# Prefetching the residual's base, finishing the last columns in PSUM, and keeping eight weight units instead of six

## The chip, the cores and the metric

One core of a Trainium2 chip runs the whole kernel. The metric is device time in microseconds; the number of a version is the median of its runs. TensorE (PE) does the matmuls into PSUM; VectorE (DVE), ScalarE (ACT) and GpSimd (POOL) do the elementwise work; SP, ACT and POOL issue DMA transfers. Each engine executes its own instructions in order.

## The reference

One layer: a token mixer, a residual with layer norm, a SwiGLU block, and a second residual with layer norm. The change lies in the last two lines of this cut:

```python
x = layer_norm(ALPHA * x + (1.0 + gt_m) * y, ln1_g[l], ln1_b[l])
h = x * (1.0 + sc_f) + sh_f
y = swiglu(h, w_gate[l], w_up[l], w_down[l])        # (silu(h @ w_gate) * (h @ w_up)) @ w_down
x = layer_norm(ALPHA * x + (1.0 + gt_f) * y, ln2_g[l], ln2_b[l])
```

There are 512 tokens of 2048 columns, and the SwiGLU block has 5632 hidden columns. All is float32.

## The kernel before

Each float32 product is done as three matmuls of split operands: a high part, made by ACT as a rounded copy, and a low part, made by VectorE as the difference (`split`, L276 and L277; `mm3`, L241 to L243). The gate and up products and the down product use seven block products instead of eight (`SEVEN`, `DOWN_SEVEN`), so each of the block products `p1 q7 r6 q5 p3 p2 q4` of the down projection has 22 units: 11 row groups `n` by 2 column halves `cc`. A unit is one weight of 128x1024. For each of two token tiles `t` it does 6 matmuls of 512 columns (`dn_mm`), so a unit is a step of 12 matmuls.

The loop over `steps` (at the end of `layer_kernel`) sets the order. At step s it splits the weight of step s + 3 (`prepare`), issues loads some steps ahead (`fetch_behind`, into five buffers `raw`), and does the matmuls of step s (`dn_product`). After each half of a step, six matmuls, it takes one turn of each side generator: every `yield` in `base_side` and `end_side` is one such turn. The split weights have four buffers, so ACT's `whi` for step s + 3 waits until TensorE has finished step s - 1.

`base_side` makes the second residual's left term from `d_z`, the first sublayer's sum that was stored in DRAM: for each of 4 column blocks c it loads two rows `ln` of 512 columns to all partitions and multiplies them by ALPHA (POOL), and for each of 4 token tiles t it loads a tile `z` (`base`), subtracts the mean and multiplies by the scale (VectorE, L1527), and multiplies and adds the rows (POOL, L1530 and L1531). All transfers of it stand in POOL's queue, in the order of the code. `gtf`, the row of gates, is loaded ahead of them (1 MB to all partitions). The 16 base tiles stay until they are joined.

`end_side` first waits until 16 base tiles are there, then loads the eight rows of the final norm and joins and norms columns as the products deliver them: `join` multiplies a column block by the gate, adds the base and takes the statistics; `norm` does two `scalar_tensor_tensor`s and stores.

The last `KEEP` = 6 units (product `q4`, its last 3 row groups, both halves) have buffers of their own. Their matmuls are left out of the loop and done at the end, token tile by token tile and half by half: for t = 0 first half 0 (3 units, 18 matmuls), then half 1, then t = 1. After each the column is joined on VectorE from PSUM into SBUF (L1650 to L1652). After both halves of a t the statistics are combined (`ln_scale`), and the four column blocks are normed: block 0 on ACT and POOL (L1550 to L1552), blocks 1, 2 and 3 on VectorE (L1554 and L1556).

Of the kernel before, what the change touches and what calls it, by code (L numbers as in the profile page):

```python
# [140 lines left out]
def layer_kernel(ctx, tc, ws, wa, wada, xt, x, cin, bada, lbl, ghg, gcq, gckv, ln1c, lnrow, ident, lvm, dist, out):  # L141
# [11 lines left out]
    def heap(name, dt=FT, w=T):  # L153
        return hp.tile([P, w], dt, name=name, tag="h")
# [4 lines left out]
    def big(name, dt=FR):  # L159
        return bp.tile([P, 4, T], dt, name=name, tag="big")  # L160
# [114 lines left out]
    def split(src, hi, lo, engine=nc.vector):  # L275
        nc.scalar.activation(hi, src, AF.Copy)  # L276
        engine.tensor_sub(lo, src, hi.bitcast(FT))  # L277
# [789 lines left out]
    def gate_row(n, name):  # L1067
        r = cp.tile([P, D], FT, name=name, tag="row")
        nc.gpsimd.dma_start(r, d_row[n].rearrange("k p -> (k p)").rearrange("(o d) -> o d", o=1).to_broadcast([P, D]))
        return r  # L1070
# [152 lines left out]
    def piece(w, n):  # L1223

        if isinstance(w, list):
            return w[n]
        return w[0][:, n * T:n * T + T], w[1][:, n * T:n * T + T]
# [67 lines left out]
    def prepare(step):  # L1295

        if step >= len(steps):
            return
        u = steps[step]
        g = u.group  # L1300
        r = raws.pop((g, u.i), None)
        if r is None:
            r = raws[g, OF[u.i]]
            if u.i == "r6":
                raws[g, "kept"] = r
            if u.i not in ("p1", "p2"):
                del raws[g, OF[u.i]]
        u.pair = u.place() if hasattr(u, "place") else W.pair()
        split(r, *u.pair)


    for c in range(4):
# [148 lines left out]

    def dn_mm(u, t):
        (_, n, cc), i = u.group, u.i
        whi, wlo = u.pair
        hi, lo = facts[i, n]
        at = CHAIN[i], cc, t
        fresh = n == 0 and i in FRESH + ("q4",)
        if fresh:
            acc[at] = bank(f"dn{CHAIN[i]}")
        for k in range(2):  # L1470
            s = slice(k * H + t * P, k * H + t * P + P)
            w = slice(k * T, k * T + T)
            mm3(acc[at], hi[:, s], lo[:, s], whi[:, w], wlo[:, w], fresh and k == 0,
                n == NP2 // 2 - 1 and k == 1, f=mmul, skip_group_check=True)

    def dn_product(u):
# [29 lines left out]
                del acc[CHAIN[i], cc, t]  # L1506
            del ps

    ends = []
    done = {}  # L1510
    base = {}

    def base_side():

        for c in range(4):
            rows = [heap(f"ln{n}") for n in range(2)]
            for n in range(2):
                nc.gpsimd.dma_start(rows[n], lnrow[n][:, c * T:c * T + T].to_broadcast([P, T]))
                nc.gpsimd.tensor_scalar_mul(rows[n], rows[n], ALPHA)
            yield  # L1520
            for t in range(NT):
                z = small("base")
                nc.gpsimd.dma_start(z, d_z[t, c])
                for _ in range(6):
                    yield
                base[t, c] = z
                nc.vector.tensor_scalar(z, z, mv1[t][:, 0:1], mv1[t][:, 3:4], op0=OP.subtract, op1=OP.mult)  # L1527
                for _ in range(2):
                    yield
                nc.gpsimd.tensor_mul(z, z, rows[0])  # L1530
                nc.gpsimd.tensor_add(z, z, rows[1])  # L1531
                yield

    st2 = [cp.tile([P, 24], FT, name=f"sf{t}", tag=f"st{t}") for t in range(NT)]
# [1 line left out]

    def join(t, c, y):

        nc.vector.tensor_mul(y, y, gtf[:, c * T:c * T + T])
        yield  # L1540
        nc.vector.tensor_add(y, y, base.pop((t, c)))
        yield
        nc.vector.bn_stats(st2[t][:, c * 6:c * 6 + 6], y)
        done[t, c] = y

    def norm(t, c, mv, on_pool=False, q=None):

        z, g, b = done.pop((t, c)), rows2[0][c], rows2[1][c]
        if on_pool:
            nc.scalar.activation(z, z, AF.Identity, scale=mv[:, 3:4], bias=mv[:, 4:5])  # L1550
            nc.gpsimd.tensor_mul(z, z, g)
            nc.gpsimd.tensor_add(z, z, b)  # L1552
        else:
            nc.vector.scalar_tensor_tensor(z, z, mv[:, 0:1], g, op0=OP.subtract, op1=OP.mult)  # L1554
            yield
            nc.vector.scalar_tensor_tensor(z, z, mv[:, 3:4], b, op0=OP.mult, op1=OP.add)  # L1556
        (q or nc.sync).dma_start(out[t * P:t * P + P, c * T:c * T + T], z)

    def end_side():

        while len(base) < 16:
            yield
        for n in range(2):
            rows2.append([heap(f"l2_{n}_{c}") for c in range(4)])
            for c in range(4):
                nc.gpsimd.dma_start(rows2[n][c], lnrow[2 + n][:, c * T:c * T + T].to_broadcast([P, T]))
        for n in range(8):
            while not ends:
                yield
            for _ in join(*ends.pop(0)):  # L1570
                yield
            yield

        for t in range(2):
            for cc in range(2):
                v = part["V"][:, 2 * cc + t]
                nc.vector.tensor_mul(v, v, gtf[:, (cc + 2) * T:(cc + 3) * T])
                yield
                nc.vector.tensor_add(v, v, base.pop((t, cc + 2)))
                yield  # L1580
        for t in (2, 3):
            mv = ln_scale(st2[t], "mv2")
            for c in range(4):
                for _ in norm(t, c, mv):
                    yield
                yield
        del part["Y"], part["R"]
        for n in range(4):
            while not ends:
                yield  # L1590
            for _ in join(*ends.pop(0)):
                yield
            yield


    KEEP = 6
    for u in steps[len(steps) - KEEP:]:
        u.place = lambda: (lambda w: (w[:, :2].rearrange("p a b -> p (a b)"), w[:, 2:].rearrange("p a b -> p (a b)")))(big("wkeep"))

    gtf = None  # L1600
    for step in range(len(steps)):
        u = steps[step]
        if step + 3 < len(steps):
            prepare(step + 3)
        fetch_behind(step)
        for ahead, do in ((4, factor_tiles), (8, factor_load)):
            if step + ahead < len(steps):
                v = steps[step + ahead]
                if v.group[0] == "dn" and v.group[2] == 0:
                    do(v.i, v.group[1])  # L1610
        last = step >= len(steps) - KEEP
        if u.group[0] == "gu":
            gu_product(u)
            gu_use(u)
        elif not last:
            dn_product(u)
            dn_use(u)
        add_behind(step)
        if not last:
            u.pair = None  # L1620
        if step == 3 * NPRE + 2:
            for t in range(NT):
                side.drain(t)
            assert not hraw
        if u.group[0] == "gu" and u.group[1] >= NPRE and u.i in ("q7", "q5"):

            nc.gpsimd.tensor_copy(pace, acc_copy[0])
            more(1)
        if step == nsteps - 1:
            del m_hi, m_lo  # L1630
            mh = None
            sums.clear()
            xp.release()
            yp = ctx.enter_context(tc.tile_pool(name="tail", bufs=24, side="right", reuse_waits="tile"))
            small = lambda name, dt=FT: yp.tile([P, T], dt, name=name, tag="y")
            for i in "EYVR":
                part[i] = big(i, FT)
            gtf = gate_row(1, "gtf")
            side.add(0, base_side())
            side.add(1, end_side())  # L1640
    side.drain(0)
# [2 lines left out]
    for t in range(2):  # L1644
        for cc in range(2):
            for u in steps[len(steps) - KEEP:]:
                if u.group[2] == cc:
                    dn_mm(u, t)
            ps, y, v = acc.pop(("Y", cc, t)), heap("y"), part["V"][:, 2 * cc + t]
            nc.vector.tensor_mul(y, ps, gtf[:, (cc + 2) * T:(cc + 3) * T])  # L1650
            nc.vector.tensor_add(y, y, v)
            nc.vector.bn_stats(st2[t][:, (cc + 2) * 6:(cc + 3) * 6], y)  # L1652
            done[t, cc + 2] = y
        mv = ln_scale(st2[t], "mv2")
        for c in (0, 1, 2, 3):
            for _ in norm(t, c, mv, c == 0, nc.scalar if c == 0 else nc.sync):
                pass


# [101 lines left out]
```

## Time and profile before

| | |
|---|---|
| median of 3 runs | 2802.89 us (2801.14 to 2803.51) |
| profiled execution | 2800.09 us, span 2798.0 us |
| busy in it | PE 98%, VectorE 73%, ACT 41%, POOL 24% |
| mean granted clock of TensorE | 0.995 |

The span is the time from the first to the last instruction of the profiled execution; all times below count from its start. A busy share is a mean over the whole span. In a timeline, the brackets behind a row give the idle time of the engine before that instruction and what ended it.

### The profile page before, as it was taken

The page shows a single profiled execution, that of the slowest core. Times are in us where ns is not written, and L with a number is a line of the kernel's source. Part 1 is how long each engine was busy: PE and PEld are TensorE (multiplying, and loading weights), DVE is VectorE, ACT ScalarE, POOL GpSimd, SP SyncE. Part 2 cuts the span into 40 slices and gives each one's busy share as a digit, 9 for nine tenths or more (in the row PEclk, how much of TensorE's full clock was granted, in tenths as well). Part 3 has the DMA queues.
Part 4 walks back from the last instruction along what each step waited for, and adds up shares of the span by engine and source line. Part 5 has one row for each costly group of instructions (what it writes and reads, how often), then busy time and mean ns, then how long its engine had stood idle before and what let it go on. Part 6 is the DMA issues. An engine that isn't in the chain of part 4 may idle for free.

```text
span 2798.0 us, 41846 instructions
## 1 busy us (share of the span) xinstructions
PE 2750.3 (98%) x16090; PEld 2421.6 (87%) x16090; DVE 2040.0 (73%) x2892; ACT 1158.3 (41%) x1724; POOL 675.6 (24%) x911
## 2 busy tenths in 40 slices
PE   8999999999999999999999999999999998999997
PEld 6878888888888888788889999999999998887886
DVE  7877687778862678545767777777777776776697
ACT  4334434242322556222236444444444444554453
POOL 0011132433010575421210212221222213443000
PEclk9999999999999999999999999999999999999999
DMA  9866545555984896996945556665556677888774
GB/s 381 310 212 207 167 159 176 173 178 187 320 287 144 231 283 209 271 282 188 282 156 174 182 188 178 190 183 179 197 177 194 174 189 229 274 277 276 242 257 157
DMA packets 179273, 609.85 MB, mean 218 GB/s; under 512 B 23201, under 2 KB 23505, under 8 KB 176001
## 3 DMA queue, kind: packets, MB, share of 16 engines
q1 hardware_dynamic: 126866, 430.18, 44.8%
q0 software_dynamic: 51776, 176.44, 23.5%
q8 instruction: 126, 2.06, 0.3%
q14 instruction: 73, 0.60, 0.1%
q10 hardware_dynamic: 432, 0.57, 0.1%
HBM read 564.09 MB, written 149.70 MB: 255 GB/s over the span
## 4 chain that ended last, share of the span: by engine, by line
PE 90%; DVE 4%; DMA 3%; issue 2%; ACT 1%; POOL 1%; SPq 0%; DVEq 0%; POOLq 0%; ACTq 0%
PE gb L233 6%; PE y L233 6%; PE ga L233 6%; PE V L243 6%; PE V L241 6%; PE V L242 6%; PE qb L233 3%; PE pb L233 3%; PE g L233 3%; PE v L233 3%; PE Y L241 3%; PE Y L243 3%; PE Y L242 3%; PE pa L233 3%; PE early L233 2%; PE dnV L242 2%
## 5 line engine op out<-in xcount | busy, mean ns | idle before, releaser
L277 DVE TENSOR_TENSOR wlo<-raw,whi 128x1024 fp32r<-128x1024 f32 x376 | 468.4, 1253 | 235.4 <-ACT whi L276 235.3
L276 ACT ACTIVATE whi<-raw 128x1024 fp32r<-128x1024 f32 x376 | 397.5, 1058 | 345.2 <-PE dnV L243 132.8
L363 DVE TENSOR_TENSOR wlo<-raw,whi 128x1024 fp32r<-128x1024 f32 (+1 forms) x228 | 284.3, 1250 | 112.3 <-ACT whi L351 111.9
L351 ACT ACTIVATE whi<-raw 128x1024 fp32r<-128x1024 f32 (+1 forms) x228 | 233.7, 1038 | 194.8 <-DVE raw L1086 72.3
L243 PE MATMUL V<-mhi,wlo 128*128 128x256 f32 x1056 | 298.7, 283 | 0.0
L241 PE MATMUL V<-mhi,whi 128*128 128x256 f32 x1056 | 298.6, 283 | 0.0
L242 PE MATMUL V<-mlo,whi 128*128 128x256 f32 x1056 | 298.4, 283 | 0.0
L242 PEld LDWEIGHTS V<-mlo,whi 128*128 128x128 f32 x1056 | 202.2, 191 | 0.0
L241 PEld LDWEIGHTS V<-mhi,whi 128*128 128x128 f32 x1056 | 202.2, 191 | 0.0
L243 PEld LDWEIGHTS V<-mhi,wlo 128*128 128x128 f32 x1056 | 202.2, 191 | 0.0
L241 PE MATMUL Y<-R,whi 128*128 128x256 f32 x704 | 196.1, 279 | 2.2 <-ACT whi L276 2.2
L243 PE MATMUL Y<-R,wlo 128*128 128x256 f32 x704 | 195.6, 278 | 1.8 <-DVE wlo L277 1.8
L242 PE MATMUL Y<-R,whi 128*128 128x256 f32 x704 | 195.7, 278 | 0.0
L242 PE MATMUL dnV<-wlo,fhi 128*128 128x512 f32 x352 | 139.1, 395 | 10.4 <-DVE wlo L277 10.4
L243 PE MATMUL dnV<-whi,flo 128*128 128x512 f32 x352 | 138.7, 394 | 0.0
L241 PE MATMUL dnV<-whi,fhi 128*128 128x512 f32 x352 | 137.9, 392 | 0.2 <-DVE V L1495 0.2
L241 PEld LDWEIGHTS Y<-R,whi 128*128 128x128 f32 x704 | 133.3, 189 | 2.4 <-ACT whi L276 2.4
L243 PEld LDWEIGHTS Y<-R,wlo 128*128 128x128 f32 x704 | 133.0, 189 | 2.2 <-DVE wlo L277 2.2
L242 PEld LDWEIGHTS Y<-R,whi 128*128 128x128 f32 x704 | 133.2, 189 | 0.0
L276 ACT ACTIVATE whi<-wrow 128x1024 fp32r<-128x1024 f32 x80 | 84.4, 1055 | 84.7 <-DVE wrow L1284 84.7
L997 POOL DMA_DIRECT2D sum_dn<-in_ws x132 | 97.1, 816 | 57.9 <-DMA sum_dn<-in_ws 49.6
L233 PE MATMUL ga<-hThi,whi 128*128 128x512 f32 x256 | 102.0, 398 | 0.0
(453 smaller groups left out, 7740.0 us busy)
## 6 DMA issues: line engine op xcount, KB each, us to landing
raw<-in_ws SPq DMA_DIRECT2D x414, 512.0 KB, 5.0
sum_dn<-in_ws POOLq DMA_DIRECT2D x132, 512.0 KB, 8.6
raw<-in_wada SPq DMA_DIRECT2D x128, 512.0 KB, 5.2
raw<-sum_dn SPq DMA_DIRECT2D x88, 512.0 KB, 4.8
rawb<-in_wada SPq DMA_DIRECT2D x22, 1024.0 KB, 12.0
sum_dn<-sum_dn POOLq DMA_DIRECT2D x44, 512.0 KB, 4.9
wrow<-in_ws SPq DMA_DIRECT2D x40, 512.0 KB, 6.6
sum_gu<-in_ws POOLq DMA_DIRECT2D x24, 512.0 KB, 9.4
```

What stands on the lines that cost most here:

```text
L233: mmul(*a, **k)
L241: f(ps, ahi, bhi, start=first, stop=False, **k)
L242: f(ps, ahi, blo, start=False, stop=False, **k)
L243: f(ps, alo, bhi, start=False, stop=last, **k)
L276: nc.scalar.activation(hi, src, AF.Copy)
L277: engine.tensor_sub(lo, src, hi.bitcast(FT))
L351: nc.scalar.activation(hi, src, AF.Copy)
L363: nc.vector.tensor_sub(lo, src, hi.bitcast(FT))
L997: nc.gpsimd.dma_start(d_sum[g, dst], block(g, src), **({"accum_op": OP.add} if add else {}))
```

## The change

There are three parts. The base's loads are issued a column block ahead: those of block 0 at the start of `base_side`, before 16 turns without work, and those of block c + 1 before the arithmetic of block c; `gtf` is loaded behind those of block 1, and each tile takes 5 turns instead of 9. The last products' columns stay in PSUM: the join writes back to the bank that it reads, and the norm's first instruction writes to PSUM too (for block 1 to a fresh bank `n1`), the second to SBUF. And eight units are kept instead of six; the first two have eight tiles of 512 columns from the pool of the base tiles.

```diff
@@ def prepare(step):
-        split(r, *u.pair)
+        if isinstance(u.pair, list):
+            for k, (hi, lo) in enumerate(u.pair):
+                split(r[:, k * T:k * T + T], hi, lo)
+        else:
+            split(r, *u.pair)
@@ def dn_mm(u, t):
-            mm3(acc[at], hi[:, s], lo[:, s], whi[:, w], wlo[:, w], fresh and k == 0,
+            mm3(acc[at], hi[:, s], lo[:, s], *piece(u.pair, k), fresh and k == 0,
@@
+    def base_load(c):
+        rows = [heap(f"ln{n}") for n in range(2)]
+        zs = [small("base") for t in range(NT)]
+        for n in range(2):
+            nc.gpsimd.dma_start(rows[n], lnrow[n][:, c * T:c * T + T].to_broadcast([P, T]))
+        for t in range(NT):
+            nc.gpsimd.dma_start(zs[t], d_z[t, c])
+        return rows, zs
+
     def base_side():
+        rows, zs = base_load(0)
+        for _ in range(16):
+            yield
         for c in range(4):
-            rows = [heap(f"ln{n}") for n in range(2)]
             for n in range(2):
-                nc.gpsimd.dma_start(rows[n], lnrow[n][:, c * T:c * T + T].to_broadcast([P, T]))
                 nc.gpsimd.tensor_scalar_mul(rows[n], rows[n], ALPHA)
-            yield
+            now, nowz = rows, zs
+            if c < 3:
+                rows, zs = base_load(c + 1)
+            if c == 0:
+                gtf.append(gate_row(1, "gtf"))
             for t in range(NT):
-                z = small("base")
-                nc.gpsimd.dma_start(z, d_z[t, c])
-                for _ in range(6):
-                    yield
+                z = nowz[t]
                 nc.vector.tensor_scalar(z, z, mv1[t][:, 0:1], mv1[t][:, 3:4], op0=OP.subtract, op1=OP.mult)
-                for _ in range(2):
-                    yield
-                nc.gpsimd.tensor_mul(z, z, rows[0])
-                nc.gpsimd.tensor_add(z, z, rows[1])
+                yield
+                yield
+                nc.gpsimd.tensor_mul(z, z, now[0])
+                nc.gpsimd.tensor_add(z, z, now[1])
+                base[t, c] = z
+                yield
+                yield
                 yield
@@
-    KEEP = 6
-    for u in steps[len(steps) - KEEP:]:
-        u.place = ...
+    KEEP = 8
+    def keep_big():
+        w = big("wkeep")
+        return [(w[:, k], w[:, 2 + k]) for k in range(2)]
+    def keep_small():
+        return [(small("wkhi", FR), small("wklo", FR)) for k in range(2)]
+    for n, u in enumerate(steps[len(steps) - KEEP:]):
+        u.place = keep_small if n < 2 else keep_big
@@ at the end, for each t and cc
-            ps, y, v = acc.pop(("Y", cc, t)), heap("y"), part["V"][:, 2 * cc + t]
-            nc.vector.tensor_mul(y, ps, gtf[:, (cc + 2) * T:(cc + 3) * T])
+            y, v = acc.pop(("Y", cc, t)), part["V"][:, 2 * cc + t]
+            nc.vector.tensor_mul(y, y, gtf[0][:, (cc + 2) * T:(cc + 3) * T])
             nc.vector.tensor_add(y, y, v)
@@ at the end, for each t
-        for c in (0, 1, 2, 3):
-            for _ in norm(t, c, mv, c == 0, nc.scalar if c == 0 else nc.sync):
-                pass
+        ys = {c: done.pop((t, c)) for c in range(4)}
+        g, b = rows2
+        z = ys[0]
+        nc.scalar.activation(z, z, AF.Identity, scale=mv[:, 3:4], bias=mv[:, 4:5])
+        for c in (1, 2, 3):
+            y = bank("n1") if c == 1 else ys[c]
+            nc.vector.scalar_tensor_tensor(y, ys[c], mv[:, 0:1], g[c], op0=OP.subtract, op1=OP.mult)
+            if c == 1:
+                nc.gpsimd.tensor_mul(z, z, g[0])
+                nc.gpsimd.tensor_add(z, z, b[0])
+                nc.scalar.dma_start(out[t * P:t * P + P, :T], z)
+                o = ys[1]
+            else:
+                o = heap("y")
+            nc.vector.scalar_tensor_tensor(o, y, mv[:, 3:4], b[c], op0=OP.mult, op1=OP.add)
+            nc.sync.dma_start(out[t * P:t * P + P, c * T:c * T + T], o)
```

POOL's queue at the start of the down products, behind the last store of the hidden activations. Before:

```order
L1069 DMA gtf<-d_row 128x2048
L1518 DMA ln_22587<-in_lnrow 128x512
L1519 TENSOR_SCALAR ln_22587<-ln_22587 128x512
L1518 DMA ln_22588<-in_lnrow 128x512
L1519 TENSOR_SCALAR ln_22588<-ln_22588 128x512
L1523 DMA base<-d_z 128x512
L1530 TENSOR_TENSOR base<-base,ln_22587 128x512
L1531 TENSOR_TENSOR base<-base,ln_22588 128x512
```

And with the change:

```order
L1520 DMA ln_22585<-in_lnrow 128x512
L1520 DMA ln_22586<-in_lnrow 128x512
L1522 DMA base<-d_z 128x512 x4
L1532 TENSOR_SCALAR ln_22585<-ln_22585 128x512
L1532 TENSOR_SCALAR ln_22586<-ln_22586 128x512
L1520 DMA ln_22770<-in_lnrow 128x512
L1520 DMA ln_22771<-in_lnrow 128x512
L1522 DMA base<-d_z 128x512 x4
L1069 DMA gtf<-d_row 128x2048
L1543 TENSOR_TENSOR base<-base,ln_22585 128x512
```

Six loads now stand ahead of the first multiply, where a load, a multiply, a load and a multiply stood ahead of the first `z`; `gtf` went from first place to behind twelve loads.

VectorE at the same place, from its last instruction of the gate and up products (the first row) to its first on `base`. Before:

```order
L1441 TENSOR_TENSOR r<-act,r 128x256
L277 TENSOR_TENSOR wlo<-raw,whi 128x1024
L277 TENSOR_TENSOR flo<-raws,fhi 128x512
L277 TENSOR_TENSOR wlo<-raw,whi 128x1024 x2
L277 TENSOR_TENSOR flo<-raws,fhi 128x512
L277 TENSOR_TENSOR wlo<-raw,whi 128x1024
L1527 TENSOR_SCALAR base<-base,mv_11710 128x512
```

And with the change:

```order
L1445 TENSOR_TENSOR r<-act,r 128x256
L277 TENSOR_TENSOR wlo<-raw,whi 128x1024
L277 TENSOR_TENSOR flo<-raws,fhi 128x512
L277 TENSOR_TENSOR wlo<-raw,whi 128x1024 x2
L277 TENSOR_TENSOR flo<-raws,fhi 128x512
L277 TENSOR_TENSOR wlo<-raw,whi 128x1024 x2
L277 TENSOR_TENSOR flo<-raws,fhi 128x512
L277 TENSOR_TENSOR wlo<-raw,whi 128x1024 x2
L277 TENSOR_TENSOR flo<-raws,fhi 128x512
L277 TENSOR_TENSOR wlo<-raw,whi 128x1024 x2
L277 TENSOR_TENSOR flo<-raws,fhi 128x512
L1540 TENSOR_SCALAR base<-base,mv_11710 128x512
```

Nine `wlo` stand ahead of the first `base` instead of four. Each belongs to one step.

VectorE at the end of the program, the norm of the first token tile (`E` and `y` lie in SBUF, `dnY` and `n` in PSUM, `l` are the rows of the final norm). Before:

```order
L1554 SCALAR_TENSOR_TENSOR E<-E,mv_25966,l_0_1_24227 128x512
L1556 SCALAR_TENSOR_TENSOR E<-E,mv_25966,l_1_1_24235 128x512
L1554 SCALAR_TENSOR_TENSOR y<-y,mv_25966,l_0_2_24228 128x512
L1556 SCALAR_TENSOR_TENSOR y<-y,mv_25966,l_1_2_24236 128x512
L1554 SCALAR_TENSOR_TENSOR y<-y,mv_25966,l_0_3_24229 128x512
L1556 SCALAR_TENSOR_TENSOR y<-y,mv_25966,l_1_3_24237 128x512
```

And with the change:

```order
L1679 SCALAR_TENSOR_TENSOR n_25978<-E,mv_25972,l_0_1_23679 128x512
L1687 SCALAR_TENSOR_TENSOR E<-n_25978,mv_25972,l_1_1_23687 128x512
L1679 SCALAR_TENSOR_TENSOR dnY<-dnY,mv_25972,l_0_2_23680 128x512
L1687 SCALAR_TENSOR_TENSOR y<-dnY,mv_25972,l_1_2_23688 128x512
L1679 SCALAR_TENSOR_TENSOR dnY<-dnY,mv_25972,l_0_3_23681 128x512
L1687 SCALAR_TENSOR_TENSOR y<-dnY,mv_25972,l_1_3_23689 128x512
```

The number and the order of the instructions are the same; from the second on each reads one operand from PSUM where it read both from SBUF.

## Rows read from the trace of the kernel before

**Rows 1.** The page: span, and busy time of each engine.
```profile
span 2798.0 us, 41846 instructions
PE 2750.3 (98%) x16090; PEld 2421.6 (87%) x16090; DVE 2040.0 (73%) x2892; ACT 1158.3 (41%) x1724; POOL 675.6 (24%) x911
```

**Rows 2.** Waits, 2200 to 2560: us in total, times, longest us.
```profile
DVE base L1527 <- DMA base<-d_z: 38.7, 8, 15.1
...
PE dnV L242 <- DVE wlo L277: 10.4, 3, 8.0
```

**Rows 3.** Timeline of TensorE: start, duration, instruction, idle time before it.
```profile
2345.22 0.39 PE L241 MATMUL dnV<-whi,fhi 128*128 128x512 f32 x1
...
2364.45 0.39 PE L241 MATMUL dnV<-whi,fhi 128*128 128x512 f32 x1
2372.84 0.80 PE L242 MATMUL dnV<-wlo,fhi 128*128 128x512 f32 x1 [8.01 <-DVE wlo L277]
...
2376.61 0.40 PE L242 MATMUL dnV<-wlo,fhi 128*128 128x512 f32 x1
...
2765.05 0.39 PE L241 MATMUL dnY<-wkeep,fhi 128*128 128x512 f32 x1
...
2781.30 0.40 PE L243 MATMUL dnY<-wkeep,flo 128*128 128x512 f32 x1
```

**Rows 4.** Windows: busy us of each engine, granted clock, DMA share, GB/s.
```profile
2370.00:2380.00 10.00, 7.16 (x24) 5.84 (x25) 8.89 (x8) 1.58 (x2) 4.24 (x3) 0.69 0.60 193
```

**Rows 5.** Timeline of VectorE: its first instruction on `base`.
```profile
2371.11 0.55 DVE L1527 TENSOR_SCALAR base<-base,mv 128x512 f32<-128x512 f32 x1 [15.13 <-DMA base<-d_z]
```

**Rows 6.** Timeline of POOL at the start of the down products.
```profile
2350.16 0.54 POOL L1069 DMA_DIRECT2D gtf<-d_row  x1
...
2361.50 1.50 POOL L1519 TENSOR_SCALAR ln<-ln 128x512 f32<-128x512 f32 x1 [10.27 <-DMA ln<-in_lnrow]
...
2368.13 0.58 POOL L1523 DMA_DIRECT2D base<-d_z  x1
```

**Rows 7.** Timeline of VectorE at the end of the span.
```profile
2773.49 0.69 DVE L1650 TENSOR_TENSOR y<-dnY,gtf 128x512 f32<-128x512 f32 x1 [1.97 <-PE dnY L243]
...
2776.63 0.74 DVE L1554 SCALAR_TENSOR_TENSOR E<-E,mv,l 128x512 f32<-128x512 f32 x1
...
2778.07 1.78 DVE L1554 SCALAR_TENSOR_TENSOR y<-y,mv,l 128x512 f32<-128x512 f32 x1
...
2793.67 0.75 DVE L1556 SCALAR_TENSOR_TENSOR y<-y,mv,l 128x512 f32<-128x512 f32 x1
```

**Rows 8.** Timeline of POOL in the same stretch.
```profile
2777.63 1.67 POOL L1551 TENSOR_TENSOR E<-E,l 128x512 f32<-128x512 f32 x1 [214.13 <-ACT E L1550]
```

**Rows 9.** DMA issues, 2345 to 2362: count, KB each, median us to landing.
```profile
raw<-in_ws SPq DMA_DIRECT2D x5, 512.0 KB, 8.0
...
ln<-in_lnrow POOLq DMA_DIRECT2D x1, 256.0 KB, 10.7
```

**Rows 10.** Timelines of ACT and of VectorE before the kept units are done.
```profile
2754.26 1.06 ACT L276 ACTIVATE whi<-raw 128x1024 fp32r<-128x1024 f32 x1 [1.69 <-PE dnY L243]
...
2762.84 2.39 DVE L277 TENSOR_TENSOR wkeep<-raw,wkeep 128x1024 fp32r<-128x1024 f32 x2
```

**Rows 11.** Instructions by tile or line: ns min/median/max, first and last start.
```profile
L277 DVE TENSOR_TENSOR wlo<-raw,whi x376: 1206/1224/2322, 1465.4 to 2755.4; 128x1024 fp32r<-128x1024 f32 x188
...
L1495 DVE TENSOR_TENSOR V<-Y,dnV x4: 674/674/676, 2538.9 to 2541.8; 128x512 f32<-128x512 f32 x4
...
L1650 DVE TENSOR_TENSOR y<-dnY,gtf x4: 675/686/690, 2769.4 to 2785.0; 128x512 f32<-128x512 f32 x4
L1651 DVE TENSOR_TENSOR y<-y,V x4: 692/692/694, 2770.1 to 2785.7; 128x512 f32<-128x512 f32 x4
```

**Rows 12.** Timeline of POOL: a base instruction beside two of VectorE's `V<-Y,dnV`.
```profile
2540.22 2.27 POOL L1531 TENSOR_TENSOR base<-base,ln 128x512 f32<-128x512 f32 x1
```

More of the change, by code (lines that the diff above doesn't have):

```diff
@@ L1463, in dn_mm @@
         (_, n, cc), i = u.group, u.i
-        whi, wlo = u.pair
         hi, lo = facts[i, n]
@@ L1471, in dn_mm @@
             s = slice(k * H + t * P, k * H + t * P + P)
-            w = slice(k * T, k * T + T)
-            mm3(acc[at], hi[:, s], lo[:, s], whi[:, w], wlo[:, w], fresh and k == 0,
+            mm3(acc[at], hi[:, s], lo[:, s], *piece(u.pair, k), fresh and k == 0,
                 n == NP2 // 2 - 1 and k == 1, f=mmul, skip_group_check=True)
@@ L1507, in dn_use @@
             del ps
-    ends = []
+    ends, gtf = [], []
     done = {}
     base = {}
+    def base_load(c):
[6 more added lines that the diff above has]
+        return rows, zs
     def base_side():
+        rows, zs = base_load(0)
+        for _ in range(16):
+            yield
         for c in range(4):
-            rows = [heap(f"ln{n}") for n in range(2)]
             for n in range(2):
-                nc.gpsimd.dma_start(rows[n], lnrow[n][:, c * T:c * T + T].to_broadcast([P, T]))
                 nc.gpsimd.tensor_scalar_mul(rows[n], rows[n], ALPHA)
-            yield
-            for t in range(NT):
-                z = small("base")
-                nc.gpsimd.dma_start(z, d_z[t, c])
-                for _ in range(6):
-                    yield
-                base[t, c] = z
-                nc.vector.tensor_scalar(z, z, mv1[t][:, 0:1], mv1[t][:, 3:4], op0=OP.subtract, op1=OP.mult)
-                for _ in range(2):
-                    yield
-                nc.gpsimd.tensor_mul(z, z, rows[0])
-                nc.gpsimd.tensor_add(z, z, rows[1])
+            now, nowz = rows, zs
[3 more added lines that the diff above has]
+                gtf.append(gate_row(1, "gtf"))
+            for t in range(NT):
+                z = nowz[t]
+                nc.vector.tensor_scalar(z, z, mv1[t][:, 0:1], mv1[t][:, 3:4], op0=OP.subtract, op1=OP.mult)
+                yield
+                yield
+                nc.gpsimd.tensor_mul(z, z, now[0])
+                nc.gpsimd.tensor_add(z, z, now[1])
+                base[t, c] = z
+                yield
+                yield
                 yield
@@ L1537, in join @@
     def join(t, c, y):
-        nc.vector.tensor_mul(y, y, gtf[:, c * T:c * T + T])
+        nc.vector.tensor_mul(y, y, gtf[0][:, c * T:c * T + T])
         yield
@@ L1544, in join, with norm @@
         done[t, c] = y
-    def norm(t, c, mv, on_pool=False, q=None):
+    def norm(t, c, mv):
         z, g, b = done.pop((t, c)), rows2[0][c], rows2[1][c]
[L1549 to L1557, printed above, removed]
+        nc.vector.scalar_tensor_tensor(z, z, mv[:, 0:1], g, op0=OP.subtract, op1=OP.mult)
+        yield
+        nc.vector.scalar_tensor_tensor(z, z, mv[:, 3:4], b, op0=OP.mult, op1=OP.add)
+        nc.sync.dma_start(out[t * P:t * P + P, c * T:c * T + T], z)
     def end_side():
@@ L1576, in end_side @@
                 v = part["V"][:, 2 * cc + t]
-                nc.vector.tensor_mul(v, v, gtf[:, (cc + 2) * T:(cc + 3) * T])
+                nc.vector.tensor_mul(v, v, gtf[0][:, (cc + 2) * T:(cc + 3) * T])
                 yield
@@ L1593, in end_side @@
             yield
-    KEEP = 6
-    for u in steps[len(steps) - KEEP:]:
-        u.place = lambda: (lambda w: (w[:, :2].rearrange("p a b -> p (a b)"), w[:, 2:].rearrange("p a b -> p (a b)")))(big("wkeep"))
-    gtf = None
+    KEEP = 8
[6 more added lines that the diff above has]
+        u.place = keep_small if n < 2 else keep_big
     for step in range(len(steps)):
@@ L1637, in layer_kernel @@
                 part[i] = big(i, FT)
-            gtf = gate_row(1, "gtf")
             side.add(0, base_side())
@@ L1654, in layer_kernel @@
         mv = ln_scale(st2[t], "mv2")
-        for c in (0, 1, 2, 3):
-            for _ in norm(t, c, mv, c == 0, nc.scalar if c == 0 else nc.sync):
-                pass
+        ys = {c: done.pop((t, c)) for c in range(4)}
[14 more added lines that the diff above has]
+            nc.sync.dma_start(out[t * P:t * P + P, c * T:c * T + T], o)
+            ys[c] = None
 def token_order():
```

## The prediction

> **What bounds the kernel now.** The page comes first: TensorE is busy for 98% of the 2798.0 us span [rows 1], so a change pays only where TensorE stands still or has finished. The list of what TensorE waited for, over the down products, names one thing: VectorE's `wlo`, three waits of 10.4 us in all, one of them 8.0 [rows 2]. The same list says what VectorE had been waiting for: `base`, loaded from `d_z`, up to 15.1 us at a time [rows 2].
>
> The timelines then give the sizes. TensorE's first down matmul starts at 2345.22, its last at 2781.30 [rows 3]. The last 72 of them, from 2765.05, have 71 intervals in 16.25 us, 0.2289 us each [rows 3]. There are 7 products x 22 units x 12 = 1848 down matmuls, so without a stall the last would start 1847 x 0.2289 = 422.7 us after the first, at 2767.9. **TensorE loses 13.4 us in this stage.** [...]
>
> Who is late there? VectorE reaches the first `base` at 2371.11 - 15.13 = 2355.98 and stands until 2371.11 [rows 5]; the `wlo` behind it in its queue come late to TensorE. POOL issued that load only at 2368.13, because it stood 10.27 us for the first `ln` row, which lay behind the 1 MB `gtf`, and again for the second [rows 6]. The transfer itself took under 3 us.
>
> Last, the tail. The final column of tokens t = 0 begins its join on VectorE at 2773.49, its first norm instruction is at 2776.63, and from there VectorE has no pause that matters until 2793.67 + 0.75 = 2794.42 [rows 7]: with two halves of work in a row it is VectorE, not TensorE, that ends last. Beside POOL's two operations a norm instruction takes 1.78 us instead of 0.74 [rows 7, 8]; the next one is as slow, in both halves. From its end to the span's end are 3.58 us for the store.
>
> **The change, part by part.**
>
> *Base loads.* POOL now issues two `ln` rows and four `z` back to back, starting where `gtf` started, 2350.16 [rows 6]. At 0.54 us an issue the first `z` is out by 2351.8. VectorE comes to it five `wlo` later, that is five steps of 12 x 0.2289 = 2.747 us: 2355.98 + 13.7 = 2369.7. The transfer has 17.9 us. In 2345 to 2362, where the DMA engines are full, `ln` landed in 10.7 us with `gtf` ahead of it [rows 9]; `z` has only two rows ahead, half a `gtf`. I take no wait. [...] Gain 13.4; at worst (every load late again) 0, and the stage holds no more.
>
> `gtf` moves behind twelve loads and two multiplies. Its first reader is the first join, after four of seven products, 4 x 22 x 2.747 = 242 us on: nothing. The eight final-norm rows now follow after 96 half steps instead of 148, 71 us earlier, and are first read after the fifth product: nothing by themselves. The base arithmetic is unchanged in number but denser, sixteen in 110 us instead of 190; that is a rival below.
>
> *Eight kept units.* TensorE's work is the same; four units instead of three per token tile and column half stand at the end. So the join of t = 0's last column starts 48 matmuls before TensorE's last start plus 0.43 (today's 2773.49 against matmul 36 from 2765.05, at 2773.06), not 36. Two more units must be split early. Today ACT is released for the last ordinary weight at 2754.26 and VectorE finishes all six kept ones at 2762.84 + 2.39 = 2765.23 [rows 10]: seven units in 11.0 us. Nine need 14.1, and as halves of 0.69 us instead of whole ones of 1.22 [rows 11] 8 x 0.16 = 1.3 more. The last unit of the first column half is the second last split, at about 13.7; TensorE comes to it after four steps and three half steps, 15.1 us. Cost nothing, covered by 1.4 us; each us beyond it is a us of TensorE.
>
> *Columns in PSUM.* The counts of VectorE's instructions stay. No row shows VectorE writing to PSUM. Below, such a write could cost nothing or even less than one to SBUF; reading it costs nothing, 0.69 us for the join's first multiply with its PSUM input against 0.69 for the add with both inputs in SBUF [rows 11]. Above, the slowest instruction of this size is 1.78 [rows 7], 1.0 more, on five writes after the last matmul: 5 us. I take 0, nearest to the reading row. [...]
>
> What it should bring is that VectorE's four instructions beside POOL have one SBUF input each. The row nearest to that is `V<-Y,dnV`, one input in PSUM: four at 674 to 676 ns, the last pair beside a POOL multiply that ran from 2540.22 to 2542.49 [rows 11, 12]. I take 0.74 to 0.75 us beside POOL as alone.
>
> *The sum.* Last matmul start 2767.9; join 0.43 later, 2768.4; first norm instruction 2776.63 - 2773.49 = 3.14 later, 2771.5; six norm instructions at 0.72 apart and 0.75 for the last, 4.35, to 2775.9; store 3.58: **2779.4, against 2798.0, a gain of 18.6**: 13.4 from the stalls, 5.2 from the tail. VectorE is free in time: t = 0 is joined at 2757.4, normed by 2764.9, the first column of t = 1 joined by 2767.0, 1.4 us before TensorE's end. Without the kept units VectorE would be that much late: of the 5.2, about 1.4 is the kept units and 3.8 the port.
>
> The profiled run took 2800.09 us, which makes 2781.5; the median of the runs, 2802.89, stands 2.8 above it, so I forecast **2784.3 us**.
>
> **The rivals.**
>
> *The tail gains half.* POOL still slows two VectorE instructions a half, 2.0 us, or PSUM writes cost something. t = 0 then ends 2.0 later, eats the 1.4 of slack, and t = 1 pays its own 2.0: 2.6 us, **2786.9**. For it: nothing shows a PSUM write. Against: the `V<-Y,dnV` rows.
>
> *Base work too dense.* In five half steps, 6.87 us, VectorE has 2.5 `wlo` at 1.22, 1.25 `flo` at 0.69 and a base at 0.55: 4.5 us. Each of two POOL operations can hold one `wlo` by 2322 - 1224 ns = 1.1 [rows 11]: 6.7. The two `ln` multiplies a block, 1.50 each [rows 6], could add 1.1 each: 28.8 us in a block of 27.5. Four blocks: 5 us too much, against about 5.9 that the weights stand ahead (three steps, 8.2, less 1.06 on ACT and 1.22). [...]
>
> *The first load is still late.* The change would not do what it says at the larger stall if `z` lands after 2369.7, 17.9 us after issue; the longest in that stretch is 10.7 [rows 9]. [...]
>
> *Bursts starve the weights: slower.* Loads come in five bursts, four of 1.5 MB and one of 2 MB, in front of `raw`. Five `raw` buffers give a weight load 5 x 2.747 - 2.3 = 11.4 us. It lands in 8.0 where the engines are full today [rows 9]. [...] For it: 8.0 is two thirds of the way to 11.4. Against: bursts are spread by POOL's own arithmetic, and the totals are the same.
>
> **How the numbers follow.** Forecast 0.62, half a tail 0.13, too dense 0.14, first load late 0.06, starved 0.05. A measurement of this kernel tells about 0.2%, 5.6 us, from no change. All but the last are faster by more: 0.95; the last splits into same 0.02 and slower 0.03. The range starts 3.8 below the forecast (the runs before spread over 2.4, a PSUM write may be cheaper) and reaches to the dense case's upper end: 2780.5 to 2791. It leaves out the first-load and the starved case and some of each edge.
>
> **What would show it.** Right: no idle TensorE from 2345 to its last matmul, near 2768; VectorE without a wait on `base`; norm instructions at 0.74 beside POOL; about 11.5 us from the last matmul's start to the span's end, today 16.7. Wrong: a TensorE gap with VectorE waiting on `base` (first load), with `wlo` at 2.3 in rows (dense), or with ACT waiting on `raw` (starved); norm instructions near 1.8 in the tail; PSUM rows well above 0.75.

## The result, and the profile after

The changed kernel takes **2783.07 us** (median of 4 runs, 2782.53 to 2785.46) against 2802.01 (4 runs of the kernel before on the same chip): a ratio of 0.9935, 95% interval 0.9918 to 0.9952. The forecast was 2784.3. By the medians the gain is 18.9 us, where 18.6 was forecast; that the two lie so close is in part luck, since the four runs of the changed kernel alone spread over 2.9 us.

The page's first lines, to hold against [rows 1]:

```profile
span 2783.5 us, 41852 instructions
...
PE 2748.0 (99%) x16090; PEld 2421.5 (87%) x16090; DVE 2047.7 (74%) x2900; ACT 1158.6 (42%) x1732; POOL 676.3 (24%) x911
```

TensorE's first and last down matmul, to hold against [rows 3] (start, duration, instruction):

```profile
2348.84 0.39 PE L241 MATMUL dnV<-whi,fhi 128*128 128x512 f32 x1
...
2771.71 0.40 PE L243 MATMUL dnY<-wkeep,flo 128*128 128x512 f32 x1
```

The prediction cut the time in two at the last matmul's start, and so does everything below. **Stage** is from the first down matmul's start to the last one's; **tail** is from there to the span's end.

| profiled execution | first | last | span | stage | tail |
|---|---|---|---|---|---|
| before | 2345.22 | 2781.30 | 2798.0 | 436.08 | 16.70 |
| after | 2348.84 | 2771.71 | 2783.5 | 422.87 | 11.79 |

The stage gave 13.2 us (predicted 13.4), the tail 4.9 (predicted 5.2). Together 18.1, near the 18.9 between the medians. In the kernel before, one stop has most of the 13.4: the gap from 2364.45 to 2372.84, 8.4 us where 0.2 is normal, and behind it nine intervals in 3.77 us where the steady rate gives 2.06 [rows 3], in 2370 to 2380 with a mean granted clock of 0.69 [rows 4]. That makes 8.2 + 1.7 = 9.9 us; the other 3.5 lie further on, around waits for `wlo` of 1.51 us at 2530 and 0.91 at 2534. The two profiled spans differ by 14.5 only, because the execution that was profiled after came to the stage 3.6 us later. Neither the change nor the stage is the cause: 2.6 of it had arisen before 445 us, in the same code, and over the fourteen profiles of this study that early point lies anywhere from 441.7 to 445.1. Hence stages and tails are compared here, not spans.

The list of waits over the whole stage (2335 to 2790: us in total, times, longest) has no row for a waiting TensorE left, and none for VectorE on a load of `base`, where [rows 2] had 10.4 and 38.7 us. POOL's waits for `base` are down from 75.3 us to 27.7, and ACT's for the loads of weights up from 8.6 to 12.2:

```profile
POOL base L1543 <- DVE base L1540: 27.7, 13, 4.6
...
ACT whi L276 <- DMA raw<-in_ws: 12.2, 7, 3.1
```

POOL's timeline shows the loads that now go out together, against [rows 6], and its operations in the tail, against [rows 8]:

```profile
2353.80 1.07 POOL L1520 DMA_DIRECT2D ln<-in_lnrow  x2
2356.19 1.59 POOL L1522 DMA_DIRECT2D base<-d_z  x3 [1.32 <-DMA d_q<-r]
...
2407.07 1.61 POOL L1543 TENSOR_TENSOR base<-base,ln 128x512 f32<-128x512 f32 x1
...
2776.30 1.26 POOL L1681 TENSOR_TENSOR E<-E,l 128x512 f32<-128x512 f32 x1 [8.37 <-ACT E L1676]
```

VectorE's timeline: its first `base` instruction, without idle time before it where [rows 5] had 15.13; one split that POOL's operation of 2407.07 holds up (0.69 alone); then the last column's join and norm, against [rows 7]:

```profile
2373.85 0.54 DVE L1540 TENSOR_SCALAR base<-base,mv 128x512 f32<-128x512 f32 x1
...
2407.44 1.79 DVE L277 TENSOR_TENSOR flo<-raws,fhi 128x512 fp32r<-128x512 f32 x1
...
2772.14 0.70 DVE L1667 TENSOR_TENSOR dnY<-dnY,gtf 128x512 f32<-128x512 f32 x1 [1.37 <-PE dnY L243]
...
2775.29 0.75 DVE L1679 SCALAR_TENSOR_TENSOR n<-E,mv,l 128x512 f32<-128x512 f32 x1
...
2776.75 0.75 DVE L1679 SCALAR_TENSOR_TENSOR dnY<-dnY,mv,l 128x512 f32<-128x512 f32 x1
2777.53 0.75 DVE L1687 SCALAR_TENSOR_TENSOR y<-dnY,mv,l 128x512 f32<-128x512 f32 x1
...
2778.99 0.75 DVE L1687 SCALAR_TENSOR_TENSOR y<-dnY,mv,l 128x512 f32<-128x512 f32 x1
```

VectorE waits 1.37 us before the last join: it is ready in time, and the join follows the last matmul's start by 0.43, as forecast. The norm instructions at 2776.75 and 2777.53 run beside POOL's and take 0.75; before, they took 1.78 [rows 7] and 1.67.

### The profile page after: what moved, and what is told of

It reads as the page before. It is cut to its first block, busy times and chain, and to the rows that moved or that the text cites. A ratio compares the mean times of both kernels' runs of the same rounds, so it can differ in the third digit from the quotient of the medians.

```text
span 2783.5 us, 41852 instructions
## 1 busy us (share of the span) xinstructions
PE 2748.0 (99%) x16090; PEld 2421.5 (87%) x16090; DVE 2047.7 (74%) x2900; ACT 1158.6 (42%) x1732; POOL 676.3 (24%) x911
## 3 DMA queue, kind: packets, MB, share of 16 engines
q8 instruction: 126, 2.06, 0.3%
## 4 chain that ended last, share of the span: by engine, by line
PE 91%; DVE 3%; DMA 2%; ACT 1%; issue 1%; POOL 1%; SPq 0%; DVEq 0%; ACTq 0%; POOLq 0%
PE gb L233 6%; PE y L233 6%; PE ga L233 6%; PE V L243 6%; PE V L241 6%; PE V L242 6%; PE pb L233 3%; PE g L233 3%; PE dnV L243 3%; PE dnV L242 3%; PE Y L243 3%; PE Y L241 3%; PE dnV L241 3%; PE v L233 3%; PE Y L242 3%; PE pa L233 3%
```

## The experiments

All stand against the kernel before, 2802.4 to 2802.6 us on the same chips. A time without an interval is that of one execution. The tail reads 11.79 to 11.87 us in all eight profiles with the changed end, and 16.70 to 16.74 in the three with the old one, so the tail resolves what the medians of single variants do not. The edits below are shown in part.

| run | time, us | ratio [95%] | stage | tail |
|---|---|---|---|---|
| loads alone | 2789.34 | 0.9951 [0.9936, 0.9966] | 422.75 | 16.74 |
| tail and kept units alone | 2797.68 | 0.9983 [0.9973, 0.9992] | 436.40 | 11.80 |
| six kept units | 2784.41 | 0.9933 [0.9915, 0.9950] | 422.75 | 13.1 |
| columns in SBUF | 2786.37 | 0.9940 [0.9925, 0.9955] | 422.87 | 13.89 |
| columns in SBUF, without POOL | 2785.08 | – | 422.87 | 11.58 |
| first block without lead | 2790.46 | 0.9960 [0.9946, 0.9974] | 430.40 | 11.85 |
| lead of 8 turns | 2783.91 | – | 422.86 | 11.8 |
| gates loaded first | 2781.51 | – | 422.86 | 11.87 |
| before, first use later | 2796.94 | – | 433.58 | 16.7 |
| 7 turns a tile | 2783.68 | – | 422.87 | 11.86 |
| 4 turns a tile | 2781.73 | – | 423.32 | 11.8 |
| 3 turns a tile | 2793.18 | 0.9963 [0.9950, 0.9976] | 431.84 | 11.84 |

### The two halves apart

The kernel before with the new `base_side` only:

```diff
+        rows, zs = base_load(0)
+        for _ in range(16):
+            yield
```

> The base's loads a block ahead, with the tail of before (six kept units, columns in SBUF). My theory: the stage of the down products, from its first matmul's start to its last, takes 422.8 us without a TensorE wait (436.1 before, 422.9 changed), the tail from the last matmul's start to the span's end stays at 16.7; in all 13.4 us less than before, ratio about 0.995. Rival (the two halves of the change need each other, or the denser base work costs TensorE time that the kept units hide): stage longer than 425 us.

And the changed kernel with the old `base_side`, and `gtf` first again:

```diff
-            rows, zs = base_load(c + 1)
+                z = small("base")
+                nc.gpsimd.dma_start(z, d_z[t, c])
+                for _ in range(6):
+                    yield
```

> Eight kept units and columns in PSUM, with the loads of before. My theory: the stage of the down products keeps its 436.1 us and VectorE its wait of about 15 us on the first base; the tail is 11.6 to 11.8 us instead of 16.7, 5 us less in all, ratio about 0.998. Rival (the tail is shorter only because the earlier part runs without stalls): tail near 16.

Measured: 13.2 and 4.8 us by the medians, 13.3 of stage and 4.9 of tail in the profiles. They add up to the whole, and neither half touches the other's part of the time. The waits of the second kernel are those of [rows 2]:

```profile
DVE base L1529 <- DMA base<-d_z: 41.7, 8, 15.0
...
PE dnV L242 <- DVE wlo L277: 10.1, 3, 7.9
```

### What in the tail does it: kept units or PSUM

```diff
-    KEEP = 8
+    KEEP = 6
@@ for n, u in enumerate(steps[len(steps) - KEEP:]):
-        u.place = keep_small if n < 2 else keep_big
+        u.place = keep_big
```

> The changed kernel with six kept units. My theory: VectorE is not free when the last matmul ends, by about 1.4 us, so the tail takes 12.8 to 13.2 us instead of 11.8 and the stage is unchanged: 1.0 to 1.4 us more than the changed kernel. Rival (kept units are worth the 2.75 us by which they bring the first join forward): 2.7 more, tail 14.5.

The tail is 13.1 us. VectorE comes to the first column of t = 1 too late and meets the last column without a wait:

```profile
2770.71 0.69 DVE L1667 TENSOR_TENSOR dnY<-dnY,gtf 128x512 f32<-128x512 f32 x1
...
2772.17 0.70 DVE L1669 BATCH_NORM_STATS2 sf<-dnY 128x6 f32<-128x512 f32 x1
2772.78 0.68 DVE L1667 TENSOR_TENSOR dnY<-dnY,gtf 128x512 f32<-128x512 f32 x1
```

Its last matmul started at 2771.00, so the join comes 1.78 after it instead of 0.43: 1.35 us later, which is the 1.3 of tail. The medians, 2784.41 and 2783.07, are too near to tell the two kernels apart.

Then eight units, with join and norm in SBUF as before:

```diff
-            nc.vector.tensor_mul(y, y, gtf[0][:, (cc + 2) * T:(cc + 3) * T])
+            nc.vector.tensor_mul(y, ps, gtf[0][:, (cc + 2) * T:(cc + 3) * T])
```

> The changed kernel with the join and the norm through SBUF tiles as before. My theory: two norm instructions a half take 1.7 to 1.8 us again beside POOL; the first half eats the slack of 1.4 us, the second pays in full: tail 14.0 to 14.5 us, 2.4 us more than the changed kernel. Rival (PSUM changes nothing but the place, the kept units make the gain): tail 11.8.

The tail is 13.89, 2.1 us more than the changed kernel's and a little under the 14.0 expected. The two norm instructions beside POOL are slow again (VectorE's timeline):

```profile
2773.74 1.75 DVE L1570 SCALAR_TENSOR_TENSOR y<-y,mv,l 128x512 f32<-128x512 f32 x1
2775.52 1.63 DVE L1572 SCALAR_TENSOR_TENSOR y<-y,mv,l 128x512 f32<-128x512 f32 x1
```

1.00 + 0.88 = 1.9 us; the last join also starts 0.87 after the last matmul instead of 0.43, because the first half had been held too. Is it POOL that holds them? The same kernel without POOL's two instructions:

```diff
             nc.scalar.activation(z, z, AF.Identity, scale=mv[:, 3:4], bias=mv[:, 4:5])
-            nc.gpsimd.tensor_mul(z, z, g)
-            nc.gpsimd.tensor_add(z, z, b)
```

> The kernel with the columns in SBUF, but with GpSimd's (POOL's) multiply and add of column block 0 left out at the end for both token tiles, so that block 0 of the output is stored unscaled. Theory (the share of the tail that the change in PSUM takes away was VectorE being held by POOL's two instructions): all norm instructions 0.74 to 0.75 us, tail from the last matmul's start to the span's end about 11.8 us, as with the columns in PSUM; down stage 422.9 us. Rival (instructions with both inputs in SBUF are slower by themselves, or a store or ScalarE holds them): two norm instructions a half still at 1.6 to 1.8 us, tail about 13.9 us.

The tail is 11.58 us, and the same two instructions, still with all their large operands in SBUF, take 0.75 (VectorE's timeline, with the join and the end of the norm):

```profile
2772.05 0.69 DVE L1669 TENSOR_TENSOR y<-dnY,gtf 128x512 f32<-128x512 f32 x1 [1.42 <-PE dnY L243]
...
2776.63 0.75 DVE L1568 SCALAR_TENSOR_TENSOR y<-y,mv,l 128x512 f32<-128x512 f32 x1
2777.41 0.75 DVE L1570 SCALAR_TENSOR_TENSOR y<-y,mv,l 128x512 f32<-128x512 f32 x1
...
2778.86 0.75 DVE L1570 SCALAR_TENSOR_TENSOR y<-y,mv,l 128x512 f32<-128x512 f32 x1
```

So the cost was VectorE being held by POOL, and one operand of each instruction in PSUM takes it away (0.75 us in the changed kernel); SBUF by itself costs nothing (0.75 without POOL). POOL gains too: its operation takes 1.26 us beside the PSUM forms, 1.64 beside the SBUF ones (first of two in the tail).

The two edits don't add: from a tail of 16.70, PSUM alone takes 3.6 us and the units alone take 2.8, both together 4.9. VectorE carries lateness from t = 0 into t = 1 only where it has no slack, and each edit makes slack.

### What in the loads does it

No lead before the first block, all else as changed:

```diff
         rows, zs = base_load(0)
-        for _ in range(16):
-            yield
```

> The changed kernel without the 16 turns ahead of the first block: the loads stand ahead as before, but VectorE comes to the first base two steps into the stage. My theory: the transfers are only one half, the place of VectorE's instruction is the other. The first base lands some 18 us into the stage (issued at 7, 11 to land), VectorE is there after 2 to 3 us, waits about 15 and TensorE loses 9 to 10 us: stage 431 to 433 us instead of 422.9, tail 11.8. Rival (the order of POOL's queue alone removes the stall): stage 422.9.

The list of waits has one of VectorE's and one of TensorE's:

```profile
DVE base L1538 <- DMA base<-d_z: 11.0, 1, 11.0
...
PE dnV L242 <- DVE wlo L277: 5.4, 1, 5.4
```

The stage is 7.5 us longer, 5.4 of it the stop itself, and in 2360 to 2380 the mean granted clock is 0.83, where 2380 to 2400 have 1.00. I had expected 9 to 10 us: the first `z` landed 7.5 us after its issue, not 11, so VectorE waited 11.0 and not 15. Half the lead:

```diff
-        for _ in range(16):
+        for _ in range(8):
```

> The changed kernel with 8 turns of lead instead of 16. My theory: VectorE comes to the first base about 13.4 us into the stage, it lands at 18, so VectorE waits about 5 us; that is within the 6 to 7 us that the split weights stand ahead, so TensorE does not stop: stage 422.9 to 424. Rival (a wait of VectorE is a wait of TensorE): stage 427 to 429.

Its list of waits:

```profile
DVE base L1540 <- DMA base<-d_z: 2.0, 1, 2.0
```

VectorE waits 2.0 us and TensorE does not notice: the split weights that stand ahead cover it. So 16 turns are more than enough. The place of `gtf`:

```diff
-            if c == 0:
-                gtf.append(gate_row(1, "gtf"))
@@ ahead of the side generators
+            gtf.append(gate_row(1, "gtf"))
             side.add(0, base_side())
```

> The changed kernel with the gate row (1 MB) loaded first again, ahead of the block of base loads. Theory (what counts is that all loads of a block are issued long before VectorE comes to them, the place of the gate row is worth nothing while there is room): the first base tiles land about 3 us later, still before VectorE comes; no wait of VectorE on base, no idle TensorE, stage 422.9 us, tail 11.8 us. Rival (the gate row ahead of the loads is what made them late): VectorE waits on base, TensorE on wlo, stage 425 to 433 us.

No wait on `base`, stage 422.86. With the loads issued early, that place costs no time. As expected the first tile landed nearly 3 us later, 19.9 us after the first down matmul against 17.3 in the changed kernel, and still ahead of VectorE, which came at 26.8.

Is it enough to move the first use, and leave every load where it was? The kernel before with

```diff
-                for _ in range(6):
+                for _ in range(16 if (t, c) == (0, 0) else 6):
```

> The kernel before with one edit: VectorE comes to the first base tile 16 turns after its load's issue instead of 6; all loads stay where they were. Theory (the first stall is only the first load being late against its use, the others are of the same kind and stay): VectorE's wait of 15 us on the first base shrinks to under 3 us and TensorE's stop near 2364 goes; the losses further on, 3.5 us, stay: stage about 426 us, tail 16.7 us. Rivals: 436 us, if the stop has another cause; 422.8 us, if the first wait alone made the later ones.

Only 2.5 us of the stage went, not 10. The first stop is gone; a VectorE wait of 4.65 us is left of the 15.13, which costs TensorE nothing. But the later loads now come late in other places: TensorE stops near 2433, 2481, 2485 and 2530, and the last of these stops is the longest. VectorE's timeline, at the first base tile and at a late one:

```profile
2374.77 0.55 DVE L1527 TENSOR_SCALAR base<-base,mv 128x512 f32<-128x512 f32 x1 [4.65 <-DMA base<-d_z]
...
2533.08 0.55 DVE L1527 TENSOR_SCALAR base<-base,mv 128x512 f32<-128x512 f32 x1 [5.56 <-DMA base<-d_z]
2533.54 1.28 DVE L1495 TENSOR_TENSOR V<-Y,dnV 128x512 f32<-128x512 f32 x2
```

And TensorE's, just behind it:

```profile
2534.37 0.77 PE L241 MATMUL dnV<-whi,fhi 128*128 128x512 f32 x1 [4.31 <-DVE V L1495]
```

Here a late `z` stands in VectorE's queue ahead of `V`, which frees the PSUM bank that TensorE wants. All three stage times that I had named were off, though the first stop went as my theory said: the rest did not stay at 3.5 us, it grew to 10.8. The edit moves all later base tiles ten turns on, so their late loads can meet other instructions in VectorE's queue, as at 2533. Mending one load's lead is not enough; with the lead on every block, in the changed kernel, no wait on `base` is left.

### How dense the base arithmetic may be

The changed kernel takes 5 turns a tile. With 7 and with 3:

```diff
@@ 7 turns
                 yield
+                yield
+                yield
@@ 3 turns
                 yield
-                yield
-                yield
```

> The changed kernel with 7 turns a base tile instead of 5. My theory: the dense base work costs nothing now, so nothing is gained: stage 422.8, tail 11.8, VectorE's busy time falls from 20.0 of 20 us to 18 or less in the base's stretch. Rival (the dense stretch costs TensorE a little in every block): stage shorter than 422.6.

> The changed kernel with 3 turns a base tile instead of 5, so 12 turns, 16.5 us, a block. POOL needs about 27 us a block beside VectorE (the blocks' multiplies start at 2374.6, 2407.1, 2434.1 and 2458.3 in the changed kernel), and a block's loads stand in its queue behind the arithmetic of two blocks earlier. My theory: the stall comes back through the loads, VectorE waits for base again in the third and fourth block, some 6 and 11 us, and TensorE loses 5 to 12 us: stage 428 to 435. Rival (VectorE, blocked by POOL at every second instruction, is simply full): TensorE waits for wlo while VectorE has no wait on base. Third (POOL's pace limits, the reserve holds): stage 423.

Seven turns change nothing, though VectorE is then busy for only 14 to 17 of each 20 us between 2380 and 2480. Three cost 9.0 us of stage, and not as my theory had it: no load was late. TensorE waited for splits in five places, while VectorE was busy without a gap (the list of waits):

```profile
PE dnY L242 <- DVE wlo L277: 5.7, 5, 2.3
```

And the windows (length, busy us of PE, PEld, DVE, ACT and POOL, granted clock, DMA share, GB/s):

```profile
2400.00:2420.00 20.00, 18.51 (x80) 14.56 (x79) 20.00 (x14) 11.04 (x14) 19.68 (x16) 1.00 0.81 271
2420.00:2440.00 20.00, 17.71 (x70) 13.87 (x69) 20.00 (x12) 7.22 (x9) 19.59 (x13) 0.91 0.81 272
2440.00:2460.00 20.00, 18.12 (x78) 14.05 (x77) 20.00 (x16) 8.64 (x10) 17.38 (x15) 1.00 0.70 221
```

My theory fell, and the rival, a full VectorE, was right. How near is the changed kernel to that? Its own windows:

```profile
2400.00:2420.00 20.00, 20.00 (x89) 16.41 (x88) 20.00 (x15) 10.99 (x15) 17.16 (x14) 1.00 0.92 311
2420.00:2440.00 20.00, 20.00 (x89) 16.40 (x88) 19.77 (x15) 9.83 (x12) 17.81 (x14) 1.00 0.86 271
2440.00:2460.00 20.00, 20.00 (x89) 16.43 (x88) 19.29 (x15) 9.76 (x12) 15.51 (x8) 1.00 0.87 306
```

Full or nearly full already, with no loss. So four turns, between the two:

> The changed kernel with 4 turns for each base tile instead of 5 (3 lost 9.0 us of TensorE). Theory (VectorE is full over the base's stretch, and what it is asked for beyond the time is lost to TensorE less a fixed reserve of the split weights): VectorE about 20.0 of 20 us in the stretch, no wait on base, TensorE waits for wlo for 3 to 6 us in all, stage 426 to 429 us, tail 11.8 us. Rival (the loss with 3 turns came from something that only the densest order has): no wait of TensorE, stage 422.9 us.

Its windows:

```profile
2420.00:2440.00 20.00, 20.00 (x89) 16.43 (x88) 20.00 (x13) 9.61 (x12) 18.59 (x15) 1.00 0.88 290
2440.00:2460.00 20.00, 19.94 (x87) 15.82 (x86) 20.00 (x16) 8.99 (x10) 17.22 (x10) 1.00 0.71 235
```

VectorE is full as expected, but TensorE loses 0.45 us, not 3 to 6. Why so much less than with three turns can be read from how far the splits stand ahead. Call *reserve* the time from the end of a step's `wlo` to the second matmul of that step, the first that reads it; steps and splits are matched by counting both in order. Where the reserve is the smallest in the changed kernel (ACT's, VectorE's and TensorE's timelines):

```profile
2385.95 1.06 ACT L276 ACTIVATE whi<-raw 128x1024 fp32r<-128x1024 f32 x1 [3.07 <-DMA raw<-in_ws]
...
2387.05 1.23 DVE L277 TENSOR_TENSOR wlo<-raw,whi 128x1024 fp32r<-128x1024 f32 x1 [1.99 <-ACT whi L276]
...
2390.27 0.39 PE L242 MATMUL dnV<-wlo,fhi 128*128 128x512 f32 x1
```

The split ends at 2388.28, so the reserve is 2.0 us. Counted over VectorE's instructions from its first `base` to POOL's last operation on one, with each instruction's time above its time alone (1.22, 0.69 or 0.54) taken as held:

| turns | stretch, us | `wlo`, `flo`, `base` | work alone | held | least reserve | stage longer by |
|---|---|---|---|---|---|---|
| 7 | 147 | 54, 26, 16 | 92.5 | 21.7 | 3.3 | 0 |
| 5 | 106 | 38, 19, 16 | 68.1 | 33.9 | 2.0 | 0 |
| 4 | 94 | 32, 16, 16 | 58.7 | 35.3 | 0.1 | 0.45 |
| 3 | 81 | 24, 12, 16 | 46.2 | 35.2 | 0.1 | 9.0 |

In all four the reserve is 5.7 to 6.0 us when VectorE comes to its first `base`. With five turns it stays at 3.0 or more through the full stretch, 2395 to 2475 (the 2.0 came before it, while weights landed late). With four it falls to 0.1 at 2444: VectorE was asked for too much here too, the reserve paid for some 5 us of it, and TensorE for the last 0.45. With three it is down to 0.1 at 2409, less than halfway, and TensorE pays for the rest. So my theory of the four-turn run, the excess less a reserve, has the right form; its sizes were off. What POOL holds up is the same 35 us with four and three turns, but it is no fixed price: 21.7 with seven turns, and 29.2 (loads alone), 29.7 (gates first), 33.9 and 36.2 (lead of 8) with five.

Four turns, or the gates loaded first, are no better kernels either: 2781.7 and 2781.5 us, of one execution each, lie within 0.2% of the changed one's 2783.07.

## Why the prediction was right, step by step

- **"TensorE loses 13.4 us in this stage"**, all of it from late loads: 13.2 came back (loads alone 13.3). The span that the steady rate gives, 422.7, was 422.75 to 422.87 in every run without a stop.
- **"The transfer has 17.9 us"**: right in substance, off in two terms. POOL's issues of `z` stood 1.32 and 0.56 us behind stores of `d_q`, so the first began 2.4 us after the first `ln`, not 1.1 (two issues of 0.54); and the four tiles of the first block took 10.0 to 11.3 us to land, where I had put them under the 10.7 of `ln`. VectorE came 17.7 us after the first issue, 7.7 after that tile had landed. The half lead, with VectorE eight turns (11.0 us) earlier, bears this out: 2.0 us of wait.
- **"Cost nothing, covered by 1.4 us"** for the eight kept units: no TensorE wait up to the last matmul.
- **"I take 0"** for PSUM writes: 0.70 in the join against 0.69, 0.75 in the norm against 0.74 or 0.75. From the last join's start to the last norm's end are 2778.99 + 0.75 - 2772.14 = 7.60 us, and 2778.86 + 0.75 - 2772.05 = 7.56 with SBUF and no POOL beside it: 0.04 us for all that the change adds in reads and writes of PSUM (the join's first multiply reads it in both). The tail's 11.79 against the forecast 11.5 is mostly the last store, 3.76 us against 3.58.
- **"VectorE's four instructions beside POOL have one SBUF input each"**: shown by the kernel with the columns in SBUF, by the same one without POOL's two instructions, and by the changed kernel, which keeps them. That one stretch shows VectorE held beside POOL, 1.75 and 1.63 us for 0.75, with all large operands in SBUF, and not held, 0.75, with one of them in PSUM.
- **"1.4 is the kept units and 3.8 the port"**: 1.3 and 3.6 in that order (before, then PSUM with six units, then eight). In the other order the units give 2.8 and PSUM 2.1, so the split holds for one order only.

Of the rivals, the half tail and the late first load did not come: no slow norm instruction, no wait on `base`.

"Base work too dense" had the right mechanism and came close: VectorE is at 20.0 of 20 us in a window of the changed kernel. The mis-sized term was "two POOL operations hold 1.1 each" plus 1.1 for each `ln` multiply. Of the 40 operations 38 lie in the stretch, 41.8 us by that price; held were 33.9. That is 7.9 us less than priced, more than the 5 us by which the sum overran. The other term, the 5.9 us that the weights stand ahead, is the reserve as measured. The upper end of the range, 2791, rests on my estimate of up to 7 us for this case, a stop and slow matmuls behind it. No run shows that term: TensorE lost nothing with five turns, 0.45 us with four and 9.0 with three, 5.7 of these in five waits for `wlo`.

"Bursts starve the weights" put the threshold at a landing time of 11.4 us. In 2360 to 2385 seven `raw` loads landed in a median 13.9 us, the slowest in 15.2, and ACT waited for `raw` seven times in the stage, 12.2 us in all. (One more wait, 4.11 us before 2379.22, the list puts down to TensorE; the load of 2365.12 landed 13.99 later, at 2379.11.) TensorE never stopped. The step of this rival that failed is the threshold: it left out the weights that are split already. A load that lands in 15.2 is 3.8 us over 11.4, and the reserve did fall by 4.0 us, from 5.95 to 1.99. At that point it is this load alone that sets it: issued at 2370.61, it landed at 2385.84, ACT began on it at 2385.95 and VectorE at 2387.05, as shown above. With the reserve counted in, the estimate of the threshold is 11.4 + 5.9 = 17.3; no run here reached it. So the changed kernel came nearest to a stop here, by the rival that had the smallest chance, and not where VectorE is full.

## What to carry to other kernels

Where an in-order engine serves a stream that the bottleneck needs, look at what stands in its queue ahead of that stream: one load issued just before its use stopped TensorE for 8.0 us here, though the transfer took under 3, and mending the first such load alone left 10.8 of the 13.3 us lost, in other places, so give the whole series a lead. Where two engines hold each other up while both work on SBUF, try one large operand of each instruction in PSUM, if it is there already: here VectorE's norm took 0.75 us instead of 1.75 and 1.63, and POOL's operations 1.26 instead of 1.64 and 1.59. And before packing side work closer, look at how far its results stand ahead of their use: the excess eats that reserve first, at no cost in time, and the bottleneck loses only what is left of it.

## What the runs showed of the hardware that I had not expected

- A POOL multiply or add of 128x512 takes 1.26 us beside VectorE's PSUM forms in the tail and 1.59 to 1.67 beside its SBUF ones; in the loop, where VectorE works on SBUF operands, the medians of the base's two are 2.2 and 1.9. What it takes from VectorE grew with the density (21.7 us with 7 turns) up to 35 us with 4 and 3 turns, and with 5 it differed by up to 7 us between runs (29.2 to 36.2).
- A PSUM write by VectorE, in place in the bank that it reads, costs at most 0.01 us on 128x512: 0.70 us in the join against 0.69 into SBUF, 0.75 in the norm against 0.74 or 0.75.
- With the DMA engines full or nearly (share 1.01 in 2360 to 2380, 0.86 to 0.92 in 2400 to 2460), a 256 KB base tile lands in 7.8 to 12.1 us, where the kernel before had 2.9 to 5.8; the weights' loads slow to a median 13.9 us in 2360 to 2385, and ACT's waiting for them costs TensorE nothing.
